# Strassen down products: split operands emitted two per tile in the direct round, and one or two per product

## The chip, the cores and the metric

The kernel runs on one core of one Trainium2 chip. The core has TensorE (matmuls, PE in the profile; PEld is its loading of weights), VectorE (DVE), ScalarE (ACT), GpSimd (POOL) and SyncE (SP), which here only issues transfers. The metric is device microseconds of one execution; a comparison is made between medians of executions of both kernels on the same chip.

## The reference, cut to what matters

One inference step of a two-layer backbone on 256 context tokens and 1024 latent tokens, model width 1024, float32. Each layer ends in a gated ConvFFN; the change lies in its last product, `@ w_down`.

```python
def conv_ffn(h, w_up, conv_w, conv_b, w_down):
    u, g = jnp.split(h @ w_up, 2, axis=-1)
    u = dwconv3(u, conv_w, conv_b)
    return (jax.nn.gelu(u) * g) @ w_down          # (tokens, 2816) @ (2816, 1024)
...
    xs = xs + g2s * conv_ffn(hs, ffn_w_up[i], ffn_conv_w[i], ffn_conv_b[i], ffn_w_down[i])
```

## The kernel before

Everything lies transposed: channels on the 128 partitions, tokens along the free axis. Both token groups stand in one row of 1288 columns (`TXX`), whose halves of 644 (`NH`) are treated as left and right. The hidden width 2816 is 22 chunks of 128, the model width 8 chunks, x0 to x7.

A float32 product is made of three passes of a faster format. Each factor is split into a high part (rounded on ScalarE) and a low part (the rest, subtracted), and high x high, high x low and low x high are summed in PSUM. For a weight block, `prepare` (L224, L225) makes `hi` on ScalarE and `lo` on GpSimd; for an operand, `split_to` (L401, L402) makes the high part on ScalarE and the low part on VectorE, both named `dop`.

The down product of a layer (`down`) has three parts:

1. The direct round: hidden chunks 0 and 1 against all eight output chunks, one tile (`dn_tile`, `acc_d`) per output chunk m. VectorE adds each tile into x of that chunk (`gate_add`, L412), after that x has come back from DRAM (`reload`, L711). Two accumulators alternate.
2. The Strassen products: hidden chunks 2 to 17 in three groups of 3, 3 and 2 chunk pairs (`DN_GROUPS`). For every group and every pair of output chunks (mp = 0 to 3) seven products q stand in the order 1, 2, 6, 5, 7, 3, 4; each sums over the 3 (or 2) chunks of its group, in three passes, over two PSUM banks (L754). After a product a gate (`gate`, L740) on VectorE adds PSUM into x; the gates of one accumulator stand between its products, so that the third product waits for the gate of the first. Weight sums (s1, s2, s4) are made on VectorE from four raw blocks a11, a12, a21, a22, which SyncE loads (L168).
3. The last four hidden chunks, direct again.

The operands of part 2 were written to DRAM by the up product (`fD`). `jobs` lists 68 of them in the order of use: 4 of the direct round, 56 of the products (operands 4 to 59), 8 of the last part. `pump(k)` emits up to k jobs: the load into one of four staging tiles (`fst`, L693; loads run up to four jobs ahead) and the two halves of the split. Split operands live in a ring of 26 places (`NRING`), and a job is emitted only when the place that it takes has been read by a group's last pair of output chunks (`freed`). So operands 4 to 25 fit beside the direct round, and those of group 1 and group 2 come while mp = 3 of the group before frees places.

TensorE and SyncE run in the order in which the code is written. The order on the other engines is chosen by a scheduler from the code's order and what each instruction waits for. `unit()` (called before each product) prepares weights until four units are ready (`top_up`). So on SyncE the loads of raw weights, of x and of staged operands stand in one queue, and each staged load waits until VectorE has split what lay in its staging tile.

Of the kernel before, what the change touches and what calls it, by code (L numbers as in the profile page):

```python
# [64 lines left out]
def backbone(ctx: ExitStack, tc, xT, cpk, ada_w, w_in, w_out, w_qkv, w_oa, w_ob, w_up, w_dn,  # L65
# [12 lines left out]
    def close(*cs):  # L78
        for c in cs:
            c.__exit__(None, None, None)  # L80
# [131 lines left out]
    def prepare():  # L212
        i = st["next"]
        if i >= len(order):
            return
        st["next"] += 1
        if callable(order[i]):
            raw = order[i]()
        else:
            raw = load_raw(order[i], f"{i}")  # L220
        wpool = S.wx if i >= len(order) - 5 else wp
        hi = wpool.tile([P, 512], F32R, tag="hi", name=f"hi{i}")[:, 0:raw.shape[-1]]
        lo = wpool.tile([P, 512], F32R, tag="lo", name=f"lo{i}")[:, 0:raw.shape[-1]]
        A.activation(hi, raw, AF.Copy)  # L224
        (V if i in on_dve else G).tensor_tensor(out=lo, in0=raw, in1=hi.bitcast(F32), op=ALU.subtract)  # L225
        ready.append((hi, lo))

    def top_up():
        while st["next"] < min([len(order)] + gates) and len(ready) < LOOKAHEAD + (st["next"] == len(order) - 5):
            prepare()  # L230
# [396 lines left out]
    def down(l, last):  # L627
# [62 lines left out]
        def load(j):  # L690
            if j < len(jobs) and j not in tiles:
                tiles[j] = staged()[:, 0:jobs[j][1]]
                dma(tiles[j], jobs[j][2])  # L693

        def pump(k):

            nonlocal js
            while k and js < len(jobs) and jobs[js][0] - NRING < freed:
                for j in range(js, js + 4):
                    load(j)  # L700
                jobs[js][3](tiles.pop(js))
                tiles[js] = None
                js += 1
                k -= 1
# [11 lines left out]
        for m in range(KD):  # L716
            dn_tile([chunk(0), chunk(2)], f"d{l}_0", m, lambda m, acc: gate_add(m, acc, l, 5))
            reload(m + 3)
            pump(3)
        freed = 4  # L720
        close(psa_c)
        ps3_c = open_ps3()
        j0 = 0
        BANKS = {0: ((0, NP_ + 4), (NP_ + 4, NH)), 1: ((0, NP_ + 4), (NP_ + 4, NH)), 2: ((0, NB), (NB, NH))}

        PLAN = {1: (0, True, 0, 0), 2: (1, True, 0, 0), 6: (0, False, 0, 1), 5: (2, True, 1, 1),
# [15 lines left out]
        for gi, (k0, nk) in enumerate(DN_GROUPS):  # L742
            for mp in range(4):
                sl = {}
                for q in Q_ORDER:
                    role, begin, t, half = PLAN[q]
                    if begin:
                        sl[role] = slot(j0 + role, f"dn{l}_{gi}_{mp}_{q}")
                    wh, wl = unit()
                    for k in range(nk):  # L750
                        w, d = slice(k * P, (k + 1) * P), places[first[gi, q] + k]
                        for pi, (ww, o) in enumerate(((wh, 0), (wh, NH), (wl, 0))):
                            for b, (a, e) in enumerate(BANKS[role]):
                                T.matmul(sl[role][:, b, 0:e - a], ww[:, w], d[:, o + a:o + e],  # L754
                                         start=begin and k + pi == 0, stop=k == nk - 1 and pi == 2,
                                         skip_group_check=not begin)
                    gate(2 * mp + t, half, sl[role], BANKS[role])
                    if mp == 3:
                        freed += nk
                    pump(3)  # L760
                j0 += 1
        pump(len(jobs))
        fin = [chunk(total + 2 * i) for i in range(4)]
# [912 lines left out]
```

## Time and profile before

| | us |
|---|---|
| median of three executions | 3124.16 (3119.94 to 3126.88) |
| the profiled execution | 3124.16, of which 3122.3 from the first to the last instruction |
| TensorE busy | 3000.8 (96%) |
| VectorE busy | 1737.8 (56%) |
| ScalarE busy | 1223.3 (39%) |
| GpSimd busy | 924.3 (30%) |
| mean granted TensorE clock | 0.985 of full |

Matmuls are pipelined, so that a busy TensorE need not be at its peak; a stretch of the down stage is best read by how many matmuls it holds. The down stage of layer 0 runs from about 1130 to 1390 us of the span, that of layer 1 from about 2792 to 3052.

### The profile page before, as it was taken

The numbers are of one execution on the slowest core, as the hardware profiler recorded it, in microseconds if no ns is written. First come the engines' busy times: TensorE is split into PE (matmuls) and PEld (weight loads), VectorE is DVE, ScalarE is ACT, GpSimd is POOL, SyncE is SP. The second block draws the span as 40 slices with busy tenths as digits, with TensorE's granted clock in tenths as the row PEclk, the third lists the DMA queues.
The fourth block names the chain that finished last, engine by engine and source line by source line (L and its number), as shares of the span: only waits on it lengthen the run. The fifth ranks groups of instructions, "written<-read, shape, count | busy, mean of one in ns | idle before, by whom it ended". The sixth has DMA issues, their size and how long they took to land. (4 is left out here: it accounts for less than half of the span.)

```text
span 3122.3 us, 49357 instructions
## 1 busy us (share of the span) xinstructions
PE 3000.8 (96%) x19149; PEld 2709.0 (87%) x19149; DVE 1737.8 (56%) x2725; ACT 1223.3 (39%) x2082; POOL 924.3 (30%) x887
## 2 busy tenths in 40 slices
PE   8999999999999989999999999999899999998998
PEld 5776788899999979988887888878899999998997
DVE  5432336865454466663365555665884555546665
ACT  4111113643333333334355555553653333433333
POOL 2111121044444423334212212211034444433334
PEclk9999999899999999999999999999999999999999
DMA  6745412232222254423544444566332223245432
GB/s 213 208 141 194 140 55 99 81 113 83 90 99 76 91 202 121 123 82 108 137 132 128 126 130 132 166 182 219 122 107 90 98 77 104 71 145 165 130 89 88
DMA packets 221640, 387.10 MB, mean 124 GB/s; under 512 B 37134, under 2 KB 107022, under 8 KB 221406
## 3 DMA queue, kind: packets, MB, share of 16 engines
q1 hardware_dynamic: 163695, 290.11, 31.0%
q10 hardware_dynamic: 57711, 93.83, 8.2%
q8 instruction: 151, 2.47, 0.3%
q14 instruction: 83, 0.68, 0.1%
HBM read 285.53 MB, written 99.05 MB: 123 GB/s over the span
## 5 line engine op out<-in xcount | busy, mean ns | idle before, releaser
L225 POOL TENSOR_TENSOR lo<-raw,hi 128x512 fp32r<-128x512 f32 x154 | 208.8, 1359 | 840.8 <-ACT hi L224 786.1
L754 PE MATMUL dn<-dop,hi 128*128 128x322 f32 (+2 forms) x1792 | 349.2, 318 | 32.3 <-ACT hi L224 12.0
L754 PEld LDWEIGHTS dn<-dop,hi 128*128 128x128 f32 x1792 | 299.6, 194 | 38.6 <-ACT dop L401 22.7
L225 POOL TENSOR_TENSOR lo<-raw_a,hi 128x512 fp32r<-128x512 f32 x154 | 217.3, 1411 | 296.2 <-ACT hi L224 296.2
L224 ACT ACTIVATE hi<-raw 128x512 fp32r<-128x512 f32 x186 | 115.9, 628 | 422.7 <-DMA raw<-w_in 121.5
L740 DVE SCALAR_TENSOR_TENSOR x<-dn,mod,x 128x384 f32<-128x384 f32 (+4 forms) x288 | 165.0, 602 | 120.4 <-PE dn L754 120.2
L224 ACT ACTIVATE hi<-raw_a 128x512 fp32r<-128x512 f32 x160 | 100.7, 629 | 321.4 <-PE u L992 159.9
L754 PE MATMUL dn<-dop,lo 128*128 128x260 f32 (+2 forms) x896 | 210.9, 317 | 2.8 <-POOL lo L225 2.7
L225 POOL TENSOR_TENSOR lo<-ra_a,hi 128x512 fp32r<-128x512 f32 x80 | 135.1, 1688 | 137.9 <-ACT hi L224 137.9
L754 PEld LDWEIGHTS dn<-dop,lo 128*128 128x128 f32 x896 | 164.2, 194 | 5.1 <-POOL lo L225 5.1
L1493 ACT ACTIVATE p<-p,ng 128x640 f32<-128x640 f32 x128 | 106.0, 828 | 155.6 <-DVE ng L1491 155.1
L225 POOL TENSOR_TENSOR lo<-raw_dn_a,hi 128x384 fp32r<-128x384 f32 (+1 forms) x96 | 95.6, 996 | 217.3 <-ACT hi L224 217.3
L1506 ACT ACTIVATE ptb<-pt 128x256 f32<-128x256 f32 (+1 forms) x288 | 110.3, 422 | 79.8 <-PE pt L1505 73.2
L401 ACT ACTIVATE dop<-fst 128x644 fp32r<-128x644 f32 (+1 forms) x136 | 99.8, 740 | 85.4 <-DMA fst<-fD 62.4
L1491 DVE CUSTOM_DVE_ANT_0 p<-sc,bt 128x640 f32<-128x640 f32 x128 | 105.4, 823 | 43.1 <-PE sc L1489 33.4
L402 DVE TENSOR_TENSOR dop<-fst,dop 128x644 fp32r<-128x644 f32 (+1 forms) x136 | 114.6, 862 | 26.1 <-ACT dop L401 25.7
L300 PE MATMUL a_q<-xh,hi 128*128 128x512 f32 (+1 forms) x456 | 120.4, 370 | 1.4 <-DVE t L1289 0.6
L300 PE MATMUL a_q<-xh,lo 128*128 128x512 f32 (+1 forms) x456 | 117.6, 366 | 0.0
L300 PE MATMUL a_q<-xl,hi 128*128 128x512 f32 (+1 forms) x456 | 117.5, 366 | 0.0
L1505 PE MATMUL pt<-ck,p 128*128 128x128 f32 x704 | 105.1, 274 | 7.3 <-DVE vts L1305 5.8
L1446 POOL TENSOR_TENSOR k<-kd,k 128x512 fp32r<-128x512 f32 x48 | 61.9, 1318 | 166.7 <-ACT k L1445 123.0
L1505 PEld LDWEIGHTS pt<-ck,p 128*128 128x128 f32 x704 | 85.4, 141 | 28.5 <-DVE vts L1305 7.3
(335 smaller groups left out, 7947.0 us busy)
## 6 DMA issues: line engine op xcount, KB each, us to landing
adau<-ada_w SPq DMA_DIRECT2D x80, 512.0 KB, 4.5
fD<-y ACTq DMA_DIRECT2D x112, 322.0 KB, 4.0
fst<-fD SPq DMA_DIRECT2D x112, 322.0 KB, 3.6
raw_a<-w_up SPq DMA_DIRECT2D x80, 256.0 KB, 2.7
ra_a<-w_up SPq DMA_DIRECT2D x80, 256.0 KB, 2.9
x<-xS SPq DMA_DIRECT2D x24, 642.0 KB, 6.8
raw<-w_in SPq DMA_DIRECT2D x48, 256.0 KB, 4.2
raw<-w_qkv SPq DMA_DIRECT2D x48, 256.0 KB, 3.0
```

Source lines behind the costliest of these rows:

```text
L224: A.activation(hi, raw, AF.Copy)
L225: (V if i in on_dve else G).tensor_tensor(out=lo, in0=raw, in1=hi.bitcast(F32), op=ALU.subtract)
L300: T.matmul(acc[:, g, 0:nn] if hasattr(acc, "shape") else acc[g][:, 0:nn], ww, aa[:, o:o + nn], start=first and pi == 0, stop=last and pi == 2)
L401: A.activation(hi, src, AF.Copy)
L402: V.tensor_tensor(out=lo, in0=src, in1=hi.bitcast(F32), op=ALU.subtract)
L740: V.scalar_tensor_tensor(out=o, in0=i0, scalar=g[r], in1=o, op0=ALU.mult, op1=ALU.add)
L754: T.matmul(sl[role][:, b, 0:e - a], ww[:, w], d[:, o + a:o + e], start=begin and k + pi == 0, stop=k == nk - 1 and pi == 2, skip_group_che ...
L1446: G.tensor_tensor(out=k2[:, o:o + 512], in0=kd[:, o:o + 512], in1=k1.bitcast(F32)[:, o:o + 512], op=ALU.subtract)
L1491: V.tensor_tensor_reduce(out=pp, in0=sc[:, 128:768], in1=btt[rh][:, CT[j], :], scale=1.0, scalar=MASK, op0=ALU.add, op1=ALU.min, accum_out=ng)
L1493: A.activation(pp, pp, AF.Exp, scale=-1.0, bias=ng, accum_out=sm)
L1505: T.transpose(pt[:, e, :], p[:, c * P:(c + 1) * P], ident)
L1506: A.activation(ptb[:, cs[0]:cs[0] + len(cs), :], pt[:, 0:len(cs), :], AF.Copy)
```

## The change

```diff
--- before.py
+++ after.py
@@ -716,11 +716,12 @@
         for m in range(KD):
             dn_tile([chunk(0), chunk(2)], f"d{l}_0", m, lambda m, acc: gate_add(m, acc, l, 5))
             reload(m + 3)
-            pump(3)
+            pump(2)
         freed = 4
+        top_up()
         close(psa_c)
         ps3_c = open_ps3()
-        j0 = 0
+        j0 = step = 0
         BANKS = {0: ((0, NP_ + 4), (NP_ + 4, NH)), 1: ((0, NP_ + 4), (NP_ + 4, NH)), 2: ((0, NB), (NB, NH))}
 
         PLAN = {1: (0, True, 0, 0), 2: (1, True, 0, 0), 6: (0, False, 0, 1), 5: (2, True, 1, 1),
@@ -757,7 +758,9 @@
                     gate(2 * mp + t, half, sl[role], BANKS[role])
                     if mp == 3:
                         freed += nk
-                    pump(3)
+
+                    step += 1
+                    pump(2 if mp in (0, 3) and step % 2 else 1)
                 j0 += 1
         pump(len(jobs))
         fin = [chunk(total + 2 * i) for i in range(4)]
```

Fewer jobs are emitted at a time: two instead of three after each tile of the direct round, and one or two instead of three after each product (two after every other product of mp = 0 and mp = 3). At the end of the direct round `top_up` is called once. After the direct round 20 jobs have been emitted instead of 26; the products' operands still are all emitted before the first product that reads them. No instruction is added or removed, and TensorE's and GpSimd's orders are the same in both kernels. In both layers the same rows move.

SyncE in the direct round of layer 0, in one piece of the difference (a staged load is `fst<-fD`; the rows of `x` are x3, x4, x5, x6 in turn, x7 follows after two or three more):

```order
 L711 DMA x_9671<-xS 128x1284
-L693 DMA fst<-fD 128x644 x3
+L693 DMA fst<-fD 128x644 x2
 L711 DMA x_9662<-xS 128x1284
-L693 DMA fst<-fD 128x644 x3
-L168 DMA raw_dn_0_a_9798<-w_dn 128x384
+L693 DMA fst<-fD 128x644 x2
+L168 DMA raw_dn_0_a_9788<-w_dn 128x384
 L711 DMA x_9663<-xS 128x1284
-L693 DMA fst<-fD 128x644 x3
+L693 DMA fst<-fD 128x644 x2
 L711 DMA x_9664<-xS 128x1284
```

Before each x there stands one staged load fewer than the time before: x6 now comes after 9 instead of 12, x7 after 11 instead of 15.

VectorE at the end of the direct round, layer 0, before (from the addition of tile 7 into x7; `x0<-dn0_0_0_1` is the gate of the first product):

```order
L412 SCALAR_TENSOR_TENSOR x7_9661<-acc_d0_0_7_10005,mod_75,x7_9661 128x1024
L402 TENSOR_TENSOR dop0_19_9948<-fst_9910,dop0_19_9948 128x644
L402 TENSOR_TENSOR dop0_20_9953<-fst_9915,dop0_20_9953 128x644
L402 TENSOR_TENSOR dop0_21_9958<-fst_9920,dop0_21_9958 128x644
L402 TENSOR_TENSOR dop0_22_9992<-fst_9946,dop0_22_9992 128x644
L402 TENSOR_TENSOR dop0_23_9997<-fst_9951,dop0_23_9997 128x644
L740 SCALAR_TENSOR_TENSOR x0_9668<-dn0_0_0_1_10035,mod_75,x0_9668 128x256
L402 TENSOR_TENSOR dop0_24_10002<-fst_9956,dop0_24_10002 128x644
L740 SCALAR_TENSOR_TENSOR x0_9668<-dn0_0_0_1_10035,mod_75,x0_9668 128x384
```

and after the change:

```order
L412 SCALAR_TENSOR_TENSOR x7_9661<-acc_d0_0_7_9970,mod_75,x7_9661 128x1024
L402 TENSOR_TENSOR dop0_15_9928<-fst_9890,dop0_15_9928 128x644
L402 TENSOR_TENSOR dop0_16_9962<-fst_9895,dop0_16_9962 128x644
L402 TENSOR_TENSOR dop0_17_9967<-fst_9921,dop0_17_9967 128x644
L402 TENSOR_TENSOR dop0_18_9993<-fst_9926,dop0_18_9993 128x644
L402 TENSOR_TENSOR dop0_19_9998<-fst_9960,dop0_19_9998 128x644
L741 SCALAR_TENSOR_TENSOR x0_9668<-dn0_0_0_1_10009,mod_75,x0_9668 128x256
L741 SCALAR_TENSOR_TENSOR x0_9668<-dn0_0_0_1_10009,mod_75,x0_9668 128x384
```

The gate of the first product still stands behind five splits, but of operands 15 to 19, no longer 19 to 23, and its two halves are no longer parted by a split.

SyncE at the end of group 0, from the weights of mp = 3 on, before (`raw_dn_0_a` are a11 and a12, `ra_dn_0_a` a21 and a22, of the first pair of group 1):

```order
L693 DMA fst<-fD 128x644 x12
L168 DMA raw_dn_0_a_10760<-w_dn 128x384
L693 DMA fst<-fD 128x644 x3
L168 DMA raw_dn_0_a_10801<-w_dn 128x384
L168 DMA ra_dn_0_a_10803<-w_dn 128x384
L168 DMA ra_dn_0_a_10805<-w_dn 128x384
L693 DMA fst<-fD 128x644 x6
```

and after the change (`raw_dn_1_a` is a11 of the second pair):

```order
L693 DMA fst<-fD 128x644 x6
L168 DMA raw_dn_0_a_10730<-w_dn 128x384
L693 DMA fst<-fD 128x644
L168 DMA raw_dn_0_a_10761<-w_dn 128x384
L168 DMA ra_dn_0_a_10763<-w_dn 128x384
L168 DMA ra_dn_0_a_10765<-w_dn 128x384
L693 DMA fst<-fD 128x644 x9
L168 DMA raw_dn_1_a_10962<-w_dn 128x384
L693 DMA fst<-fD 128x644 x2
```

The first pair's a11 moves ahead of six staged loads, its other three blocks ahead of eight.

ScalarE at the same place, before (`hi250` to `hi256` are the roundings of the seven weights of group 1's first pair, `dop0_43` that of operand 43):

```order
L401 ACTIVATE dop0_43_10793<-fst_10750 128x644
L401 ACTIVATE dop0_44_10798<-fst_10755 128x644
L224 ACTIVATE hi250_10762<-raw0_dn_1_0_a11_10760 128x384
L401 ACTIVATE dop0_45_10832<-fst_10786 128x644
L401 ACTIVATE dop0_46_10837<-fst_10791 128x644
L401 ACTIVATE dop0_47_10842<-fst_10796 128x644
L224 ACTIVATE hi251_10807<-raw0_dn_1_0_a12_10801 128x384
L401 ACTIVATE dop0_48_10875<-fst_10830 128x644
L401 ACTIVATE dop0_49_10880<-fst_10835 128x644
```

and after the change:

```order
L401 ACTIVATE dop0_38_10797<-fst_10725 128x644
L224 ACTIVATE hi250_10732<-raw0_dn_1_0_a11_10730 128x384
L401 ACTIVATE dop0_39_10830<-fst_10756 128x644
L224 ACTIVATE hi251_10767<-raw0_dn_1_0_a12_10761 128x384
L401 ACTIVATE dop0_40_10860<-fst_10790 128x644
L401 ACTIVATE dop0_41_10865<-fst_10795 128x644
L401 ACTIVATE dop0_42_10895<-fst_10828 128x644
L224 ACTIVATE hi252_10804<-raw0_dn_1_0_a11_10730 128x384
```

The first weight is rounded behind operand 38 instead of 44, the second behind 39 instead of 47. At the end of group 1 the rows move in the same way.

## Rows read from the trace of the kernel before

**Rows 1.** The page: the span; busy time, share and instructions of each engine.

```profile
span 3122.3 us, 49357 instructions
...
PE 3000.8 (96%) x19149; PEld 2709.0 (87%) x19149; DVE 1737.8 (56%) x2725; ACT 1223.3 (39%) x2082; POOL 924.3 (30%) x887
```

**Rows 2.** Stretches: length, busy us and instructions (PE, PEld, DVE, ACT, POOL), clock, DMA share, GB/s.

```profile
1130.24:1164.93 34.69, 28.58 (x144) 23.52 (x145) 24.62 (x31) 12.31 (x18) 3.04 (x6) 1.00 0.93 328
1164.93:1194.69 29.76, 23.07 (x126) 22.42 (x127) 25.24 (x34) 13.10 (x23) 9.74 (x9) 0.83 0.67 213
1200.00:1220.00 20.00, 20.00 (x137) 20.00 (x137) 10.25 (x19) 4.10 (x8) 8.03 (x8) 1.00 0.19 59
1245.13:1264.44 19.31, 15.12 (x92) 13.31 (x92) 16.93 (x25) 10.40 (x17) 6.01 (x5) 1.00 0.86 272
1325.42:1345.82 20.40, 16.12 (x85) 14.68 (x85) 13.55 (x23) 7.61 (x15) 5.86 (x7) 0.83 0.52 154
2826.03:2856.39 30.36, 22.98 (x126) 22.37 (x127) 23.79 (x34) 13.75 (x23) 9.87 (x9) 0.83 0.69 220
2906.83:2926.98 20.15, 16.10 (x91) 14.83 (x91) 16.71 (x25) 10.53 (x17) 6.36 (x5) 0.92 0.82 261
2987.96:3008.28 20.32, 16.10 (x86) 14.67 (x85) 13.36 (x23) 7.60 (x15) 6.09 (x7) 0.83 0.51 150
```

**Rows 3.** Timeline of SyncE, direct round and after: start, us, what it issues.

```profile
1156.26 0.47 SPq L711 DMA_DIRECT2D x<-xS  x1
...
1162.71 0.43 SPq L711 DMA_DIRECT2D x<-xS  x1
1163.24 21.34 SPq L693 DMA_DIRECT2D fst<-fD  x14
1184.64 0.90 SPq L168 DMA_DIRECT2D raw_dn_a<-w_dn  x2
```

**Rows 4.** Timelines of VectorE and ScalarE there: start, us, what, [idle before, releaser].

```profile
1163.11 1.68 DVE L412 SCALAR_TENSOR_TENSOR x<-acc_d,mod,x 128x256 f32<-128x256 f32 x2 [1.57 <-DMA x<-xS]
...
1170.22 1.67 DVE L412 SCALAR_TENSOR_TENSOR x<-acc_d,mod,x 128x256 f32<-128x256 f32 x2
...
1175.87 0.74 ACT L401 ACTIVATE dop<-fst 128x644 fp32r<-128x644 f32 x1 [2.63 <-DMA fst<-fD]
...
1176.64 0.83 DVE L402 TENSOR_TENSOR dop<-fst,dop 128x644 fp32r<-128x644 f32 x1 [1.42 <-ACT dop L401]
1177.39 0.48 DVE L740 SCALAR_TENSOR_TENSOR x<-dn,mod,x 128x256 f32<-128x256 f32 x1
...
1178.94 0.60 DVE L740 SCALAR_TENSOR_TENSOR x<-dn,mod,x 128x384 f32<-128x384 f32 x1
```

**Rows 5.** Timeline of TensorE: first matmuls of group 0's first three products.

```profile
1164.93 0.36 PE L754 MATMUL dn<-dop,hi 128*128 128x260 f32 x1 [2.69 <-DVE x L412]
...
1172.04 1.41 PE L754 MATMUL dn<-dop,hi 128*128 128x260 f32 x4 [4.21 <-ACT dop L401]
...
1179.69 0.54 PE L754 MATMUL dn<-dop,hi 128*128 128x260 f32 x2 [2.48 <-ACT dop L401]
```

**Rows 6.** Timeline of SyncE at the end of group 0.

```profile
1234.59 13.30 SPq L693 DMA_DIRECT2D fst<-fD  x11
1247.94 0.42 SPq L168 DMA_DIRECT2D raw_dn_a<-w_dn  x1
```

**Rows 7.** Timelines of GpSimd and TensorE there: the next pair's first weight and product.

```profile
1252.45 1.24 POOL L225 TENSOR_TENSOR lo<-raw_dn_a,hi 128x384 fp32r<-128x384 f32 x1 [11.04 <-ACT hi L224]
...
1252.43 0.85 PE L754 MATMUL dn<-dop,hi 128*128 128x260 f32 x4 [1.33 <-ACT hi L224]
```

**Rows 8.** L402 on VectorE, ns min/median/max: from 1140 to 1200, from 1200 to 1400.

```profile
L402 DVE TENSOR_TENSOR dop<-fst,dop x23: 811/820/1647, 1146.5 to 1184.8; 128x644 fp32r<-128x644 f32 x23
...
L402 DVE TENSOR_TENSOR dop<-fst,dop x38: 815/828/1241, 1233.7 to 1335.5; 128x644 fp32r<-128x644 f32 x34, 128x640 fp32r<-128x640 f32 x4
```

**Rows 9.** Transfers from 1125 to 1200: count, KB each, median us to landing.

```profile
fst<-fD SPq DMA_DIRECT2D x29, 322.0 KB, 4.5
```

## The prediction

> **What bounds the kernel now.** I read the page first: TensorE is busy 3000.8 us of a span of 3122.3 us [rows 1], so a change that removes no matmul can only win back stretches in which TensorE waits or runs at its lower clock. Next I read the stretches view of the two down stages, with borders at the first matmul of a product (a product of groups 0 and 1 is 3 chunks x 3 passes x 2 banks = 18 matmuls, one of group 2 is 12). In an undisturbed stretch 137 matmuls take 20 us, 0.146 us each [rows 2]. That pitch prices the disturbed stretches, each of which holds a known count. What is lost is the stretch less its count times 0.146:
> - A, the first pair of group 0 (seven products): 29.76 - 126 x 0.146 = 11.4 us in layer 0, 30.36 - 18.4 = 12.0 us in layer 1.
> - B, from group 0 into group 1: 19.31 - 92 x 0.146 = 5.9 us and 20.15 - 91 x 0.146 = 6.9 us.
> - C, from group 1 into group 2: 20.40 - 85 x 0.146 = 8.0 us and 20.32 - 86 x 0.146 = 7.8 us.
>
> That is 25.3 + 26.7 = 52.0 us, waits and the lower clock together: the granted clock averages 0.83 in A and C, 1.00 or 0.92 in B, and 1.00 in the undisturbed row [rows 2]. The transfers are busy 0.82 to 0.93 of the time in the direct round and in B, against 0.19 undisturbed. So the loss sits exactly where operands come in bursts.
>
> What ends last there is in the timelines. In A the first product starts when VectorE has emptied tile 6 of the direct round, which itself had waited for x6, issued at 1156.26 behind the staged loads [rows 3, 4, 5]. The second product starts at 1172.04, when VectorE has emptied tile 7 (x7 was issued at 1162.71). The third starts at 1179.69, just after the gate of the first product (0.48 + 0.60 us from 1177.39), which stood in VectorE's queue behind five operand splits; the last of these waited 1.42 us for its rounding, and that 2.63 us for its transfer [rows 4, 5]. The view names ScalarE's dop for the last two waits; that had long been done for the operands these products read. In B the weights are late: SyncE issues 11 staged loads in 13.30 us before the raw weight of the next pair goes out at 1247.94, and GpSimd, which makes its low part, sits idle for 11.04 us until 1252.45 [rows 6, 7]. The product had been due when the one before it ended, at 1251.1 = 1252.43 - 1.33 [rows 7]; its low part is there at 1253.69.
>
> **The change, part by part.** No instruction is added or removed. The same 68 jobs (a load on SyncE, a rounding on ScalarE, a subtraction on VectorE) stand later in their queues, and weights and gates stand earlier; the orders of TensorE and GpSimd stay as they were.
>
> *Two per tile in the direct round.* x6 now stands behind 9 staged loads instead of 12, x7 behind 11 instead of 15. One such load is 322 KB, 0.33 MB [rows 9], and the stretch moved 328 GB/s [rows 2], so each costs 1.0 us there: x6 comes 3 us and x7 4 us earlier. The first product gains at most its own wait, 2.7 us, since the matmuls before it end at 1162.24. The second, bound by x7, starts at 1172.04 - 4 = 1168.0. The third is bound by the gate of the first, which still stands behind five splits, but the last is that of operand 19 and not 23: four transfers fewer, 1179.69 - 4 = 1175.7. From there the ten operands not yet emitted by then come two per product or one: 2 x 0.82 us of splits [rows 8] and 1.08 us of gate are 2.72 us on VectorE per product, against 18 x 0.146 = 2.63 us on TensorE. Five products take 13.6 us at that pace, and pair 1 starts at 1189.3 instead of 1194.69: **5.4 us** gained, and the same in layer 1. From below, if only the transfers before x7 count, it is 4.0; from above, all that is lost in A, 11.4. I take 5.4, because VectorE's pace is a row and the walk uses it. Pair 1's first raw weight, issued at 1184.64 [rows 3], stands behind the same 14 loads after an x7 that is 4 us earlier, and its other three blocks behind 16: two loads of 1.5 us (21.34/14) more, at about 1183.7, for a product due at 1192; it is hidden with some 5 us to spare for landing, rounding and subtraction.
>
> *One or two per product in B.* 21 splits now lie over 14 products instead of 7. On SyncE, the next pair's first weight stands behind 6 staged loads instead of 12; at 13.30/11 = 1.21 us each that is 7.3 us earlier, 1240.6 in place of 1247.94, and its low part at 1246.4 instead of 1253.69, 4.7 us before it is due. Its rounding on ScalarE moves from behind operand 44 to behind operand 38. Moved along with it are the loads of the other three blocks of the pair, which step from 15 to 7 staged loads behind, and the first weight of pair 1, from 21 to 16. VectorE then carries, per seven products (18.4 us), 10.25/20 x 18.4 = 9.4 us of other work [rows 2] and 10.5 splits of 0.83 us [rows 8], 8.7: together 18.1. It just fits. Where it doesn't, the gate is late; one product lies between a gate and the product that needs it, 2.6 us of slack. I leave 1.0 us of loss in each B: 5.9 + 6.9 - 2.0 = **10.8 us** gained. The bounds are 0 and 12.8.
>
> *The same in C.* Products of group 2 are 12 matmuls, 1.75 us, with gates as long as before. Seven products carry about 9 us of gates and weights (9.4 less what the narrower weights save) and 7 splits (5.8 us) in 12.3 us: 2.5 us too much, part of it taken by the two longer products ahead. I leave 1.5 us in each: 8.0 + 7.8 - 3.0 = **12.8 us**, between 0 and 15.8.
>
> *The weights made ready at the end of the round.* The call prepares the one unit that the first product's own call would have prepared next, with only a change of pools between; it issues no load. I cost it at nothing: if it does anything it is one rounding of about 0.5 us on ScalarE, which is busy 12.31 of 34.69 us there [rows 2].
>
> **The sum** is 2 x 5.4 + 10.8 + 12.8 = 34.4 us. The profiled execution took 3124.16 us (1.9 around its span of 3122.3) and is the median of the three runs, so it needs no correction: 3124.2 - 34.4 = **3090 us**.
>
> **The rivals.** (1) *A stays.* The direct round is bound by transfers, and what x6 and x7 gain the operands of the first products lose again: 15 splits instead of 11 now lie behind tile 7. For it: SyncE needs 21.34 us for 14 loads there [rows 3]. Against: the bytes until the third product fall by four loads. B and C alone give 23.6 us: 3101. (2) *The weights stay late.* SyncE's pace in B is set by staging buffers that splits free, and splits wait for ring places that TensorE frees, so fewer rows ahead need not mean earlier. For it: the loads went at 1.21 us apiece, not at the transfers' 1.0. Against: places come free at three per 2.63 us, 0.88 us each, faster than that. Then only A gains: 3124.2 - 10.8 = 3113; if A is as in rival 1 too, nothing changes, 3124. (3) *Slower: VectorE becomes the bound.* GpSimd's low parts now run among the splits instead of being held up until after them. One split in A took 1.647 us against a median of 0.820, 0.83 us more [rows 8]; I take that for such a meeting. If each of seven low parts per pair cost VectorE that, it would need 18.1 + 5.8 = 23.9 us for 18.4: 5.5 us lost in each of B's two pairs, 11.0 instead of 5.9 and 6.9. C, with 10 splits in its first pair and 7 in its second, would lose 23.5 - 18.4 = 5.1 and 20.6 - 12.3 = 8.3, together 13.4, instead of 8.0 and 7.8. With A unchanged that is 22.0 - 12.8 + 26.8 - 15.8 = 20.2 us more: 3144. It decides from about 0.5 us per low part: 14 x 0.5 less B's 0.6 of room is the loss B has now. Against it: over 38 splits of layer 0's B and C the median is 0.828 and the worst 1.241 [rows 8], so few were held. The Trainium skill speaks for this rival: SBUF — State Buffer, section "SBUF: two separate sides", says that a GpSimd instruction and a VectorE one with two SBUF inputs hold a shared port pair exclusively, the later one waiting for the whole instruction. By that rule, taken for every low part, the time would be that of this rival; the one split of 1.647 us agrees with it, the medians say that the two seldom meet.
>
> **How the numbers follow.** Forecast 0.60; A stays 0.20; weights late 0.12, half of it with A's gain and half with none; VectorE bound 0.08. About 0.2% (6 us) is what a measurement of this kernel can tell from no change. Faster: 0.60 + 0.20 + 0.06 = 0.86; same 0.06; slower 0.08. The range reaches down to all 52.0 us won back, 3072, and up to A's gain alone, 3113; the two cases beyond it hold 0.14.
>
> **What would show it.** Right: in B GpSimd's idle time of 11 us before the next pair's first weight is gone and the stretch from the sixth product of pair 3 to the fourth of the next takes about 14 us instead of 19.3; C takes about 14 instead of 20.4; A about 27 counted from the first product, which starts some 2.7 us sooner; the granted clock in C rises to 1.00. Wrong: TensorE's waits for gates (L740 before, L741 after) grow from the few microseconds of now to tens, VectorE's splits average near 1.2 us, or TensorE waits at pair 1 for weights that were due.

## The result, and the profile after

The changed kernel takes 3091.5 us (median of four executions, 3085.6 to 3095.6) against 3122.1 us of the kernel before on the same chip: a ratio of 0.990, 95% interval 0.988 to 0.992. The profiled execution took 3094.47 us. In the changed kernel the lines of the gates and of the products stand one further down (L741, L755).

The page after, the rows that answer to [rows 1]:

```profile
span 3092.7 us, 49333 instructions
...
PE 2987.8 (97%) x19149; PEld 2701.0 (87%) x19149; DVE 1735.3 (56%) x2725; ACT 1221.1 (39%) x2082; POOL 930.3 (30%) x887
```

Every engine has as many instructions of work as before; the 24 fewer in the first row are waits on semaphores.

The view of stretches after, with the borders of [rows 2] and the stretches between them (layer 0: direct round, A, the rest of group 0, B, the rest of group 1, C, the rest of group 2; layer 1: from A on):

```profile
1125.81:1160.68 34.87, 31.13 (x144) 25.83 (x145) 23.18 (x30) 11.00 (x16) 3.57 (x7) 0.90 0.88 316
1160.68:1187.31 26.63, 21.71 (x127) 21.25 (x126) 22.30 (x32) 13.71 (x22) 7.27 (x7) 0.87 0.75 239
1187.31:1237.75 50.44, 50.44 (x343) 50.44 (x343) 32.15 (x54) 16.50 (x29) 21.16 (x20) 1.00 0.29 90
1237.75:1251.61 13.86, 13.53 (x92) 13.30 (x92) 12.55 (x22) 8.66 (x14) 8.90 (x6) 1.00 0.75 241
1251.61:1314.76 63.15, 61.47 (x415) 61.00 (x415) 40.81 (x64) 20.47 (x36) 25.30 (x24) 1.00 0.34 110
1314.76:1328.88 14.12, 12.66 (x86) 12.31 (x85) 13.58 (x23) 7.73 (x15) 5.28 (x7) 1.00 0.63 203
1328.88:1372.68 43.80, 43.20 (x291) 42.82 (x291) 28.70 (x53) 11.88 (x26) 19.64 (x24) 1.00 0.17 49
...
2806.87:2832.71 25.84, 20.68 (x127) 20.22 (x126) 21.92 (x32) 13.91 (x22) 6.25 (x7) 0.93 0.78 250
2832.71:2884.51 51.80, 50.95 (x343) 50.48 (x343) 32.90 (x54) 16.47 (x29) 20.95 (x20) 1.00 0.29 92
2884.51:2898.29 13.78, 13.51 (x92) 13.28 (x91) 13.29 (x23) 8.83 (x15) 9.83 (x6) 1.00 0.72 229
2898.29:2961.40 63.11, 61.49 (x416) 61.03 (x415) 39.91 (x64) 20.60 (x36) 25.84 (x24) 1.00 0.34 111
2961.40:2975.38 13.98, 12.64 (x86) 12.41 (x85) 13.56 (x23) 7.54 (x15) 5.42 (x7) 1.00 0.61 202
2975.38:3021.80 46.42, 44.65 (x291) 44.24 (x290) 27.88 (x53) 11.94 (x26) 19.88 (x24) 0.96 0.16 48
```

And the rest of group 1 in the kernel before, layer 0, which the prediction had not shown because nothing was expected there:

```profile
1264.44:1325.42 60.98, 60.98 (x416) 60.98 (x415) 35.92 (x61) 18.86 (x33) 24.50 (x24) 1.00 0.28 81
```

B fell from 19.3 and 20.2 to 13.9 and 13.8 us, C from 20.4 and 20.3 to 14.1 and 14.0, A from 29.8 and 30.4 to 26.6 and 25.8. But the stretch behind B, which had been without a wait (60.98 us), grew to 63.2 and 63.1, with 4.9 us more work on VectorE than before (40.81 against 35.92): the second half of each group's splits now lies there. Below, q0, q1 and q2 are the rests of groups 0, 1 and 2.

TensorE's waits in the down stage after, layer 0, then layer 1 (us in total, times, longest):

```profile
PE dn L755 <- DVE x L741: 7.4, 5, 3.8
...
PE dn L755 <- DVE x L412: 1.2, 1, 1.2
...
PE dn L755 <- ACT hi L224: 0.4, 1, 0.4
...
PE dn L755 <- ACT dop L401: 5.2, 2, 3.5
PE dn L755 <- DVE x L741: 4.7, 4, 1.8
...
PE dn L755 <- ACT hi L224: 1.2, 3, 0.4
```

What the weights cost in B and C is gone; what is left are mostly gates on VectorE. The 5.2 us in layer 1 that the view puts down to ScalarE's `dop` are the waits of A's second and third product (1.6 and 3.5 us); these start 0.14 and 0.15 us behind tile 7's addition and the first product's gate on VectorE, as in layer 0. In A the queue of SyncE after reads, against [rows 3]:

```profile
1148.86 0.43 SPq L711 DMA_DIRECT2D x<-xS  x1
...
1155.44 0.43 SPq L711 DMA_DIRECT2D x<-xS  x1
1156.39 22.31 SPq L693 DMA_DIRECT2D fst<-fD  x14
1178.75 0.42 SPq L168 DMA_DIRECT2D raw_dn_a<-w_dn  x1
...
1181.54 0.42 SPq L168 DMA_DIRECT2D raw_dn_a<-w_dn  x1
1182.01 1.53 SPq L168 DMA_DIRECT2D ra_dn_a<-w_dn  x2
```

Counted from the first matmul of the direct round, x6 is issued at 23.1 us instead of 26.0 and x7 at 29.6 instead of 32.5. TensorE and VectorE in A after:

```profile
1160.68 0.76 PE L755 MATMUL dn<-dop,hi 128*128 128x260 f32 x4
...
1164.67 0.83 PE L755 MATMUL dn<-dop,hi 128*128 128x260 f32 x4 [1.16 <-DVE x L412]
...
1171.32 1.41 PE L755 MATMUL dn<-dop,hi 128*128 128x260 f32 x4 [3.76 <-DVE x L741]
```

```profile
1162.38 0.56 DVE L200 TENSOR_TENSOR raw_dn_a<-raw_dn_a,raw_dn_a 128x384 f32<-128x384 f32 x1
1162.85 1.67 DVE L412 SCALAR_TENSOR_TENSOR x<-acc_d,mod,x 128x256 f32<-128x256 f32 x2
1164.44 3.70 DVE L402 TENSOR_TENSOR dop<-fst,dop 128x644 fp32r<-128x644 f32 x4
1169.43 0.83 DVE L402 TENSOR_TENSOR dop<-fst,dop 128x644 fp32r<-128x644 f32 x1 [1.28 <-ACT dop L401]
1170.17 1.00 DVE L741 SCALAR_TENSOR_TENSOR x<-dn,mod,x 128x256 f32<-128x256 f32 x2
```

The first product no longer waits, the second waits for tile 7's addition, now behind four weight sums (the last of them is the first row), and the third for the gate of the first, behind the five splits that the prediction had named.

### The profile page after: what moved, and what is told of

It is laid out like the page before. It is cut to its first block, busy times and chain, and to the rows that moved or that the text cites. A ratio compares the mean times of both kernels' runs of the same rounds, so it can differ in the third digit from the quotient of the medians.

```text
span 3092.7 us, 49333 instructions
## 1 busy us (share of the span) xinstructions
PE 2987.8 (97%) x19149; PEld 2701.0 (87%) x19149; DVE 1735.3 (56%) x2725; ACT 1221.1 (39%) x2082; POOL 930.3 (30%) x887
## 3 DMA queue, kind: packets, MB, share of 16 engines
q1 hardware_dynamic: 163695, 290.11, 30.4%
## 5 line engine op out<-in xcount | busy, mean ns | idle before, releaser
L755 PE MATMUL dn<-dop,hi 128*128 128x322 f32 (+2 forms) x1792 | 342.6, 314 | 20.0 <-DVE x L741 12.1
L755 PEld LDWEIGHTS dn<-dop,hi 128*128 128x128 f32 x1792 | 294.8, 191 | 24.3 <-ACT dop L401 14.3
L741 DVE SCALAR_TENSOR_TENSOR x<-dn,mod,x 128x384 f32<-128x384 f32 (+4 forms) x288 | 162.8, 601 | 92.3 <-PE dn L755 92.2
L755 PE MATMUL dn<-dop,lo 128*128 128x260 f32 (+2 forms) x896 | 206.8, 312 | 0.0
L755 PEld LDWEIGHTS dn<-dop,lo 128*128 128x128 f32 x896 | 161.5, 190 | 0.0
L1494 DVE CUSTOM_DVE_ANT_0 p<-sc,bt 128x640 f32<-128x640 f32 x128 | 105.4, 823 | 43.1 <-PE sc L1492 34.4
L402 DVE TENSOR_TENSOR dop<-fst,dop 128x644 fp32r<-128x644 f32 (+1 forms) x136 | 116.5, 877 | 22.7 <-ACT dop L401 21.8
L1449 POOL TENSOR_TENSOR k<-kd,k 128x512 fp32r<-128x512 f32 x48 | 61.6, 1312 | 166.0 <-ACT k L1448 153.1
```

What stands on the lines that cost most here:

```text
L402: V.tensor_tensor(out=lo, in0=src, in1=hi.bitcast(F32), op=ALU.subtract)
L741: V.scalar_tensor_tensor(out=o, in0=i0, scalar=g[r], in1=o, op0=ALU.mult, op1=ALU.add)
L1494: V.tensor_tensor_reduce(out=pp, in0=sc[:, 128:768], in1=btt[rh][:, CT[j], :], scale=1.0, scalar=MASK, op0=ALU.add, op1=ALU.min, accum_out=ng)
```

## The experiments

Lengths from first matmul to first matmul in the profiled execution of each, us, mean of the two layers ("start" is direct round and A together). The kernels ran on several chips, so that medians are compared through the ratio to the kernel before on the same chip:

| kernel | median | ratio to before, 95% | start | q0 | B | q1 | C | q2 |
|---|---|---|---|---|---|---|---|---|
| before | 3122 to 3128 | | 64.3 | 50.4 | 19.7 | 61.0 | 20.4 | 43.1 |
| the change | 3091.5 | 0.988 to 0.992 | 59.5 | 51.1 | 13.8 | 63.1 | 14.0 | 45.1 |
| the change again | 3094.7 | 0.988 to 0.991 | 59.8 | 51.1 | 13.8 | 62.6 | 14.2 | 43.1 |
| without top_up | 3093.1 | 0.988 to 0.991 | 58.4 | 51.1 | 13.7 | 63.1 | 14.9 | 43.1 |
| direct round alone | 3122.9 | 0.9973 to 0.9996 | 59.2 | 52.6 | 19.9 | 61.6 | 20.9 | 43.4 |
| products alone | 3106.8 | 0.992 to 0.995 | 66.5 | 50.4 | 13.5 | 63.1 | 14.3 | 43.5 |
| weights ahead alone | 3119.2 | 0.997 to 0.998 | 67.3 | 50.4 | 20.6 | 61.0 | 15.8 | 43.1 |
| all x first | 3101.3 | 0.991 to 0.994 | 62.5 | 52.1 | 13.5 | 62.6 | 15.3 | 43.1 |
| one per tile | 3092.2 | 0.988 to 0.991 | 56.4 | 53.3 | 13.4 | 62.7 | 13.7 | 43.1 |
| two per product | 3102.9 | 0.992 to 0.994 | 60.7 | 52.7 | 16.0 | 62.3 | 14.9 | 43.7 |
| sums on GpSimd | 3097.8 | 0.990 to 0.993 | 59.5 | 50.7 | 18.1 | 61.0 | 16.4 | 42.7 |
| second pair's sums | 3092.5 | 0.986 to 0.990 | 60.0 | 51.6 | 13.8 | 61.2 | 15.3 | 43.3 |
| those, and weights ahead | 3089.9 | 0.987 to 0.990 | 59.9 | 50.4 | 13.3 | 61.6 | 14.4 | 43.4 |
| those, one per tile | 3092.6 | 0.988 to 0.991 | 57.0 | 55.4 | 13.6 | 61.4 | 14.6 | 43.1 |

**The direct round alone** (against the change):

```diff
-        top_up()
-                    pump(2 if mp in (0, 3) and step % 2 else 1)
+                    pump(3)
```

> The direct-round part alone: two per tile, three after each product, nothing made ready at the end of the round. My theory, that the places are separate (A is bound by the transfers ahead of x6 and x7, B and C by weights that stand behind staged loads): direct round and A together as in the changed kernel (61.5 us in layer 0, 57.5 in layer 1, against 64.5 and 64.2 before), B and C as before (19 to 20 us each), about 3112 us. Rival, that what A wins is lost again at B and C or the reverse: B and C change by more than 2 us.

The start falls by 5.1 us per layer (the prediction had 5.4 for A), and B and C stay within 0.6 us of before. But 2.2 us per layer come back in q0, where pair 1's weights are late (one wait of 1.6 and one of 1.3 us for a rounding). So the median is 4.9 us below that of before, and far from the 3112 expected.

**The products alone:**

```diff
-            pump(2)
+            pump(3)
-        top_up()
```

> The products' part alone: three per tile in the direct round as before, one or two after each product. My theory: B about 14 us and C about 14 us as in the changed kernel, A as before (about 30 us), the new waits behind B and C there too (2 us each after B), about 3106 us. Rival, that B and C shrink only because the direct round ends differently: B and C stay at 19 to 20 us and the time at 3122.

B and C fall by all that the change gives there, 6.2 and 6.1 us per layer, and q1 has its new waits (62.6 and 63.7 us). B and C are the larger part: 20.9 us of the median. With the 4.9 us of the direct round alone that makes 25.8, where the change gains 30.5 to 32.4. The two parts are thus not quite independent: in q0 the direct round alone loses 2.2 us per layer, the change 0.7.

**The weights ahead alone**: the kernel before, with the next pair's raw blocks loaded already before the first and before the fourth product of mp = 3.

```diff
...
+                    if mp == 3 and gi < 2 and q in (1, 5):
+                        for i in ((0, 2) if q == 1 else (1, 3)):
+                            ahead[12 * l + 4 * gi + 4](i)
```

> The kernel before, three per tile and three per product, but at the end of groups 0 and 1 the raw weights of the next pair are loaded ahead: a11 and a21 before the pair's first staged load, a12 and a22 after nine of them instead of fifteen. My theory, weights late on SyncE's queue: the wait for the weights' rounding goes from 12 us in all to under 4, B and C fall to 14 to 16 us each, about 3106 us. Rival, that the burst of 21 splits in seven products is itself too much for VectorE and the transfers, wherever the weights stand: B and C stay at 18 to 20 us, with waits for gates in place of waits for weights, and the time within 5 us of 3122.

In C the early weights alone give 4.5 and 4.7 us of the 6.3 that the change gains in its first profile. In B they give nothing, and the time is 8.5 us below before, not the 3106 expected: the waits for roundings are gone, and a gate takes their place. TensorE's waits from 1200 to 1390 us, and VectorE's queue at the longest of them (lines of the gates L748, splits L410 here):

```profile
PE dn L765 <- DVE x L748: 7.3, 3, 4.3
```

```profile
1259.04 2.38 DVE L410 TENSOR_TENSOR dop<-fst,dop 128x644 fp32r<-128x644 f32 x2
...
1261.74 1.97 DVE L410 TENSOR_TENSOR dop<-fst,dop 128x644 fp32r<-128x644 f32 x2
1263.63 1.00 DVE L748 SCALAR_TENSOR_TENSOR x<-dn,mod,x 128x384 f32<-128x384 f32 x2
```

Between these rows VectorE does not stand idle: it has no room left, and the four splits take 4.35 us instead of 3.3, with three of GpSimd's low parts beside them. So B had two causes, late weights and a VectorE that carries three splits per product; the chain of before shows only the one that ended last. The reverse, splits spread and the weights left late, was not run.

**All x first**: eight x loaded at the start of the direct round, none behind a tile.

```diff
-        for m in range(3):
+        for m in range(KD):
...
-            reload(m + 3)
```

> The changed kernel with all eight loads of x issued at the start of the direct round, ahead of the staged loads, in place of three ahead and one per tile. My theory, that the first products of A wait for tiles 6 and 7, and these for x6 and x7: no wait for L412 after the first tiles, the direct round about 31 us and A about 22 instead of 34.9/31.6 and 26.6/25.8, some 6 us less per layer, about 3079 us. Rival, that the operands' bytes bind and the x only stand in for them: the operands of the first products are late instead, direct round and A together stay within 2 us of 61.5 and 57.5, about 3091 us.

The start is 62.5 us in both layers, 3 us more than in the change, and the time lies above both expectations. SyncE issues no staged load for 14 us of the direct round of layer 0:

```profile
1137.28 5.07 SPq L693 DMA_DIRECT2D fst<-fD  x4
...
1156.72 2.54 SPq L693 DMA_DIRECT2D fst<-fD  x4
```

ScalarE has rounded the four operands in the staging tiles by 1151.8, but their splits stand on VectorE behind additions of tiles that TensorE has yet to finish, and start at 1155.87. So x's place in the queue isn't what bounds A by itself. Since the edit changed VectorE's order too, the run doesn't show how much the bytes ahead of the third product count.

**Without top_up:**

```diff
-        top_up()
```

> The change without the call of top_up at the end of the direct round; all else as in the change. My theory, as in the prediction: the call is worth nothing, so the time is that of the change, 3091 +- 4 us, with the first product, the third product and the pace behind them where the change has them (direct round and A together 61.5 us in layer 0, 57.5 in layer 1, each within 1 us). Rival: the call brings one rounding and its low part to the front of their queues, which the third product waits for; then A is longer by 0.5 to 2 us in each layer and the time 3092 to 3095.

The time lies in the ranges of theory and rival alike, but the start is no longer than with the call (58.4 us against 59.5 and 59.8): the call is worth nothing that these runs can tell, as predicted. The start came out at 57.7 and 59.2 us and not within 1 us of the first profile's: it differs as much between executions of one order, as the next run shows. **The change again:**

> The changed kernel once more, on the same chip as the three kernels beside it, so that they are compared with it and not only with the kernel before. Expected: 3091 +- 4 us; direct round and A between 57 and 62 us; the waits behind weight sums in q1 of both layers again (q1 of 62.5 to 63.5 us); B and C within 0.5 us of 13.8 and 14.1. If q1 falls to 61.0 here, those waits were an accident of one execution and the theory of the sums falls.

These two and the first profile are three executions of one order: B from 13.5 to 14.1, q1 from 62.3 to 63.5, q0 from 50.4 to 51.8, C from 13.9 to 15.6 us, and the start from 57.5 to 61.5. The waits in q1 are no accident.

**One per tile**, and three after each product of group 0's first pair:

```diff
-            pump(2)
+            pump(1)
-                    pump(2 if mp in (0, 3) and step % 2 else 1)
+                    pump(3 if gi + mp == 0 else 2 if mp in (0, 3) and step % 2 else 1)
```

> The change with one operand per tile in the direct round instead of two, and three after each of the seven products of the first pair of group 0. Theory (bytes ahead of the gates): the direct round and the start of A are set by what is transferred ahead of x6 and x7, so with 5 to 7 staged loads fewer ahead of them (1.0 us each) the first product starts some 3 us earlier than in the change, at about 32 us behind the first matmul; but 21 - 12 = 9 to 12 operands then stand among the seven products at 3 per product, 3 x 0.82 + 1.08 = 3.5 us on VectorE per product against 2.63 on TensorE, so A grows from 26.6 to about 29: the sum of both stays within 1.5 us of the change (61.5 and 57.5) and the time within 3 us of it. Rival (only the tail of the direct round counts): fewer operands behind tile 7 let the third product's gate come at once; direct and A fall by 4 us or more per layer, 3083 or less.

The third product starts 41.1 and 41.2 us behind the first matmul, against 45.5 and 42.5, and A shrinks, which the expectation had growing. Most of that is given back in q0 (53.3): TensorE waits 2.5 and 2.2 us there for pair 1's weights. The time is that of the change.

**Two per product** throughout, a dose between three and one and a half:

```diff
-                    pump(2 if mp in (0, 3) and step % 2 else 1)
+                    pump(2)
```

> The change with two operands after every product, where the change has one or two; the direct round as in the change. It is a dose between three and one-and-a-half: 21 splits of a group then end behind 10 or 11 products instead of 14. If VectorE's pace sets what is left in B and q1 (splits, gates and sums per product), the burst ends earlier and is denser: per seven products 9.4 + 14 x 0.83 = 21.0 us on VectorE for 18.4 on TensorE, so B and C rise by about 2.6 us each, to 16 and 16.5, and q1 and q2 fall back by 1 to 2 us, to 61.5 and 43.2; the time is 3091 to 3097. If the weights' place in SyncE's queue alone sets B and C, B rises with the staged loads ahead of the first weight (8 to 9 instead of 6, 1.2 us each), by 3 us, with GpSimd idle for 3 to 5 us ahead of the first low part and TensorE waiting for that rounding. If neither binds any more, the time falls by the 6 us that q1 and q2 have lost, to 3085.

B is 19.7, 16.0 and 13.8 us at three, two and one and a half splits per product, near the size worked out from VectorE's rows. TensorE's only wait in B is for a gate (layer 0; 2.7 us in layer 1), none for a rounding, though GpSimd sits idle for 5.73 us ahead of its first low part:

```profile
PE dn L755 <- DVE x L741: 2.1, 1, 2.1
```

So B here is the pace of VectorE. C (14.9) hardly moves between two and one and a half. q1 does fall, but by 0.6 us only. The ring has room for ten more operands in the first pair of group 0, as in the change, but they are emitted sooner: pair 1's first raw weight stands behind 16 staged loads instead of 14, and q0 is 52.7. With that the time is above the range.

**The sums on GpSimd** (all four of a pair, in the down products):

```diff
+        E = G if "_dn_" in nm else V
-                V.tensor_tensor(out=t["s1"], in0=t["a21"], in1=t["a22"], op=ALU.add)
+                E.tensor_tensor(out=t["s1"], in0=t["a21"], in1=t["a22"], op=ALU.add)
...
```

> The change with the four sums of a pair's weights (s1, s2's two, s4) on GpSimd instead of VectorE, in the down products alone; same values. Theory 1: what the change loses behind B and C (q1 63.2 and 63.1 against 61.0 before, q2 43.8 and 46.4 against 43.0, q0 of layer 1 51.8 against 50.4) are gates that stand on VectorE behind a pair's weight sums and a split; four sums of 0.56 us less per pair give q1 of 61.0 to 61.5, q2 of 43.1, and A shorter by 1 to 2 us, since tile 7's gate stood behind three of them: 6 to 10 us less, about 3083. Theory 2: the waits come from the splits themselves being stretched or late (transfers, roundings), not from the sums; q1 and q2 stay, and the time stays at 3091. Rival 3: GpSimd gets too slow: its subtractions of this size take 1.02 us, four more are 4.1 us per pair beside the 8.0 us in 20 that it has; the chain s1, s2, rounding, low part then ends behind the product that needs it, TensorE waits for low parts or roundings in every pair, at 1 us a pair 24 us more, about 3115.

q1 is back at 61.0 in both layers and q2 at 42.7. So the new waits are VectorE's, and without the sums there they go. But B is 17.7 and 18.5 us, and the time lies between the expectations. ScalarE, then VectorE, at the end of group 0, layer 0:

```profile
1243.79 0.53 ACT L224 ACTIVATE hi<-raw_dn_a 128x384 fp32r<-128x384 f32 x1 [2.93 <-POOL raw_dn_a L196]
1244.22 1.99 ACT L401 ACTIVATE dop<-fst 128x644 fp32r<-128x644 f32 x3
...
1244.97 2.29 DVE L402 TENSOR_TENSOR dop<-fst,dop 128x644 fp32r<-128x644 f32 x2 [2.39 <-ACT dop L401]
1247.19 1.00 DVE L741 SCALAR_TENSOR_TENSOR x<-dn,mod,x 128x256 f32<-128x256 f32 x2
```

ScalarE stands 2.93 us in front of the rounding of a sum that GpSimd makes late; three operand roundings queue behind it, VectorE idles 2.39 us, and its gates come behind those splits. TensorE then waits 2.25 us and runs part of the stretch at half clock (mean 0.90 and 0.91).

**The second pair's sums alone on GpSimd** (mp = 1 of each group):

```diff
+        E = G if "_dn_" in nm and nm.endswith("_1") else V
...
```

> The change with the weight sums on GpSimd for the second pair of output chunks (mp = 1) of each group alone; same values. These are made while the first pair is computed, beside the last splits, and in the change TensorE waited there for gates that stood behind them. With all sums on GpSimd, q1 and q2 were back at 61.0 and 42.8 us, but B and C were 3 to 4 us longer, since ScalarE's roundings of operands stood behind the rounding of a sum that GpSimd made late. If both readings hold, this kernel has the change's B and C (13.8 and 14.1, within 0.5 us) and q1 and q2 of 61.0 to 61.6 and 42.8 to 43.1: 3 to 6 us less than the change on the same chip, without the 3.4 us of half clock in layer 1's q2. Rival 1: the waits in q1 come from the late splits, not the sums; q1 and q2 stay near 63 and 43.8, and so does the time. Rival 2: the second pair's sums on GpSimd are late as well, and hold up ScalarE's roundings in mp = 0; then the waits move into B's end or q1 and the time rises by 2 to 6 us.

q1 is 61.3 and 61.0, and B stays at 14.2 and 13.5: both readings hold in these stretches. But C in layer 1 was 16.3 us and q0 51.7 and 51.5, so that little is left in the time: 2.2 us below the change on the same chip, inside its interval.

**Those, and group 0's second pair loaded ahead:**

```diff
...
+                    if mp == gi == 0 and q in (1, 5):
+                        for i in ((0, 2) if q == 1 else (1, 3)):
+                            ahead[12 * l + 1](i)
```

> The kernel before this one, and with the raw weights of group 0's second pair loaded after the first and the fourth product of its first pair, ahead of 10 and 5 staged loads more than in the change. In the change TensorE waited for those weights' roundings, 0.4 + 0.4 us in layer 1 (pair 1's weights were not hidden with 5 us to spare, as the prediction had it). Theory: these waits go, q0 is 50.44 in both layers, worth 1 to 2 us in all; A stays within 1 us of the kernel before this one, since two blocks of 0.2 MB ahead of its last operands are about 1.2 us of transfers. Rival: the blocks delay the operands of the first pair, whose gates stand behind the splits: A grows by 1.5 us or more in each layer and the time is 1 to 3 us above the kernel before this one.

q0 is 50.44 in both layers, so pair 1's weights were the wait there; A is not longer in the mean of the layers. The median is the lowest of all (its ratio is not), 4.7 us below the change on the same chip, but the two intervals overlap: faster than the change is not shown. **Those, with one per tile:**

> The second pair's sums on GpSimd, its raw weights in group 0 loaded ahead, and one operand per tile in the direct round with three after each product of the first pair. With one per tile alone A's seven products were done 2 to 4 us sooner (55.7 and 57.1 us behind the first matmul, against 57.5 and 61.5) but pair 1's weights came late (waits of 2.5 us in each layer, q0 53.3). Theory: with the weights ahead those waits go: direct, A and q0 together 107 to 108 us in both layers against 112.0 and 109.3 in the change; with q1 and q2 at 61.0 to 61.6 and 42.8 to 43.1 the time is 6 to 10 us less than the change on the same chip. Rival: the two blocks ahead take the place of the operands they overtake, the products of A wait for splits instead; direct, A and q0 stay at 109 to 110 and the gain is that of the sums alone, 3 to 6 us.

The rival, and worse: the time is 2.1 us below the change on the same chip, and in layer 0 TensorE waits 4.97 us at 1194 for a gate. It is the chain of the sums on GpSimd again: ScalarE waits 2.85 us for a sum there, and three operands' roundings stand behind it.

## Why the prediction was right, and where its steps were not

The forecast was 3090 us by a gain of 34.4; measured were 30.5 us less than before here, 32.4 and 31.3 in the other comparisons (change without top_up, change again). By terms, from the means of the three executions against the one profile of before, both layers together:

- **A with the direct round: 10.2 us gained, forecast 10.8, by two errors that cancel.** x6 came 3 us sooner, as worked out, x7 2.8 instead of 4. The first product's wait is gone, but it starts only 1.0 us sooner in the mean of the six direct rounds, not 2.7: four of them have 3.4 or 6.8 us at half clock (granted 0.90 in layer 0 of the first profile), those of before none. The start of the third product was put at 45.5 us behind the first matmul; it was 45.5 and 42.5, 43.9 in the mean of six, behind the five splits named. The five products from there were put at 13.6 us, VectorE's pace; they took 14.9 to 16.0, as before the change (15.0 and 14.9). TensorE doesn't wait between them, but 3.4 to 5.8 us of them are at half clock, behind the wait for the third product's gate: the walk put the clock there at nothing. That pair 1 started at 59.2 in the mean, forecast 59.1 in layer 0 and 58.8 in layer 1, is luck.
- **B: 11.9 us gained, forecast 10.8**, by the step named: the queue of SyncE and GpSimd's first low part of the next pair, after:

```profile
1232.56 0.38 SPq L168 DMA_DIRECT2D raw_dn_a<-w_dn  x1
```

```profile
1236.99 1.36 POOL L225 TENSOR_TENSOR lo<-raw_dn_a,hi 128x384 fp32r<-128x384 f32 x1 [2.75 <-ACT hi L224]
```

The idle 11.04 us [rows 7] are 2.75, and the product that needs it starts at 1243.64. But the reasoning was incomplete: early weights alone gain nothing in B, and the splits had to be spread as well.

- **C: 12.0 us gained, forecast 12.8.** The granted clock is 1.00 in all three executions, as said.
- **top_up: nothing**, as said.
- **Not in the sum: 6.6 us lost in q0, q1 and q2** (1.4, 3.9 and 1.3; that of q2 in one execution alone). This is the step that failed: the prediction let a burst end where its stretch ended. The splits now run on into the products where the next pair's sums are made. VectorE at 1257 us in the changed kernel, then GpSimd and TensorE:

```profile
1257.26 1.45 DVE L402 TENSOR_TENSOR dop<-fst,dop 128x644 fp32r<-128x644 f32 x1
1258.63 1.37 DVE L190 TENSOR_TENSOR s_dn<-ra_dn_a,ra_dn_a 128x384 f32<-128x384 f32 x1
1260.03 0.56 DVE L195 TENSOR_TENSOR ra_dn_a<-raw_dn_a,ra_dn_a 128x384 f32<-128x384 f32 x1
1260.51 1.00 DVE L741 SCALAR_TENSOR_TENSOR x<-dn,mod,x 128x260 f32<-128x260 f32 x2
```

```profile
1257.02 2.56 POOL L225 TENSOR_TENSOR lo<-raw_dn_a,hi 128x384 fp32r<-128x384 f32 x2 [1.38 <-ACT hi L224]
...
1261.65 0.82 PE L755 MATMUL dn<-dop,hi 128*128 128x260 f32 x4 [1.26 <-DVE x L741]
```

The gate at 1260.51 stands behind a split and two sums, and the product at 1261.65 waits 1.26 us for it. Beside GpSimd's two low parts the split took 1.45 us and not 0.82, the first sum 1.37 and not 0.56: 1.4 us more together. It is so in all six stretches of the change's order: the split and the two sums in front of that gate take 1.4 to 1.5 us more than their 0.82, 0.56 and 0.56, and the wait is 1.1 to 1.6 us. So the wait needs the split and the sums in one place, and is as long as what GpSimd adds to them: a part of rival 3, at a place where it was not looked for. Moving the sums to GpSimd takes away both at once, so that no run here parts them. With the sums elsewhere the stretch is 61.0 to 61.8 us in the four kernels that have that, eight stretches; in the three executions of the change's order it is 62.3 to 63.5 in six.
- **Pair 1's weights in group 0** were to be hidden with 5 us to spare. SyncE took 22.31 us for the 14 loads, and not 21.34 [rows 3], and the other three blocks went out at 1181.5 to 1183.5, 55.7 us behind the first matmul and not 53.5. The spare was gone: layer 1 waits 0.4 us twice, and of the kernels with two operands per tile and the burst spread, the one that loads them ahead has no wait in q0 in either layer.

The three terms come to 34.1 us, less 6.6 for the waits: 27.4 us of the down stages. The median gained 3 to 5 us more. Two things on record can make that up. The kernel with the weights ahead alone has the same order as before up to q0, and its start is 67.3 us where the one profile of before has 64.3; by the mean of both, A's gain would be 13.2 us and not 10.2. And the stretches ahead of, between and behind the down stages, which the change leaves alone, were 2604.5 us long in the profile of before, 2601.2 in the mean of the change; over all fourteen kernels of the table they lie between 2596.6 and 2604.5, so that before has the longest. Part of that is the clock (20.5 us at half clock ahead of the first down stage in the change, 27.3 before). With one profile of each kernel neither can be told from chance. So the total is nearer to the forecast than its terms are: one was missing, and that something made up for it is luck.

Of the rivals, A did not stay and the weights did not stay late. VectorE did not become the bound of B and C by collisions: over the 38 splits of layer 0 behind 1200 us the median is 0.822 us and the worst 1.653. The sign named for that, TensorE's waits for gates, grew from 4.2 to 12.1 us in all and not to tens. In B it is GpSimd that is stretched most. Its low parts and VectorE's splits, after, at the first products of group 1:

```profile
1246.15 2.17 POOL L225 TENSOR_TENSOR lo<-s_dn,hi 128x384 fp32r<-128x384 f32 x1
1248.29 3.16 POOL L225 TENSOR_TENSOR lo<-ra_dn_a,hi 128x384 fp32r<-128x384 f32 x1
1251.41 1.01 POOL L225 TENSOR_TENSOR lo<-raw_dn_a,hi 128x384 fp32r<-128x384 f32 x1
```

```profile
1248.28 2.29 DVE L402 TENSOR_TENSOR dop<-fst,dop 128x644 fp32r<-128x644 f32 x3
...
1251.45 1.65 DVE L402 TENSOR_TENSOR dop<-fst,dop 128x644 fp32r<-128x644 f32 x1
```

The low part that starts 0.01 us behind three splits takes 3.16 us instead of 1.01, and the split that starts 0.04 us behind a low part takes 1.65 instead of 0.82. The rule that the prediction cited from the Trainium skill (SBUF — State Buffer, section "SBUF: two separate sides"), that the later one waits for the whole instruction, fits the second row: 0.83 us are most of the low part. The first row goes further: the 2.15 us more are about all three splits (2.29 us), not one. So VectorE is not always the one that pays, as rival 3 had it. In B it is mostly GpSimd, which has 5 us in 13.86 idle, so TensorE doesn't see it; in q1 it is VectorE, and TensorE waits.

## What to carry to other kernels

When a burst of work is spread, ask at its far end what it meets there: here the next pair's sums on VectorE, with low parts on GpSimd beside them, and 2 us per stretch that had been clean. A stretch that is late can have two causes of which the view names one; take away the named one alone before the whole gain is put down to it (B: nothing, C: most of it). And moving work to an idler engine moves its lateness into every in-order queue that reads its result: sums on GpSimd freed VectorE and stopped ScalarE.

## What was not expected of the hardware

GpSimd's subtraction of 128x384, 1.01 us alone, took 2.17 and 3.16 us beside splits, while the splits' median stayed at 0.822; VectorE's sum of that size, 0.56 us alone, took 1.37 beside one. And the clock: in the two down stages the profiles have 37.5 us at half clock before, 20.5 in the first profile of the change and in its second, and 10.2 without top_up, with TensorE waits of 44.1, 28.9, 25.5 and 28.0 us in sum (both counted from the trace). From before to the change fewer waits went with less half clock, among the change's executions they did not, and where it falls differs between executions of one order: the direct round of layer 0 was granted 0.90 in the first profile of the change and A of layer 1 0.93.
